# Eight weight pieces move to GpSimd's DMA queue, and one block of a matrix-vector product moves from TensorE to VectorE

## The chip, the cores and the metric

The kernel runs on one core of a Trainium2 chip. The metric is the device time of one execution in microseconds, as the median of three runs. All profiles are of one execution each.

## The reference, cut to what matters

The reference is one inference step of a two-layer network for two groups of tokens: 128 context tokens and 512 latent tokens, model width 2048, all in float32. Each layer does the following (the mixers, two kinds of attention and a gated convolution in the first layer, are left out here):

```python
def modulation(cond, w, b):                      # w: (2048, 6144)
    m = jax.nn.silu(cond) @ w + b
    return jnp.split(m, 3, axis=-1)              # shift, scale, gate

sh, sc, gt = modulation(c, ada_w[layer], ada_b[layer])
h = rms_norm(x, norm_g[layer]) * (1.0 + sc) + sh
out = mixer(h, ...)                              # begins with h @ w_in, w_in: (2048, 6656)
x = x + gt * out
```

There are two conditions, `c` for the latent tokens and `c_ctx` for the context tokens, so the modulation is a product of a 2 x 2048 matrix with 2048 x 6144 weights (48 MB for each layer), of which every weight is used once for each condition. `h` cannot be made before shift and scale of its rows are known.

## The kernel before

Tokens lie along the free axis (640 of them, `NT`), features on the 128 partitions, so a feature block of 128 rows of `h` is one tile `h0` to `h15`. Matmuls of the projections are split in three float32r products (`wh*hi`, `wh*lo`, `wl*hi`, lines 276 to 278); `split_w` makes `wh` on ScalarE (line 241) and `wl` on VectorE (line 242) from a loaded tile `raw`.

The modulation weights are cut in blocks of 512 columns (`cb`): blocks 0 to 3 are the shift, 4 to 7 the scale, 8 to 11 the gate. Block `g` and block `4 + g` belong to quarter `g` of the features (four `h` tiles). In layer 0 the shift and scale blocks are made by `ada_on_pe`: TensorE multiplies 16 slices of the block (line 178, `T<-ada,sT`), ScalarE copies the result (line 181), TensorE transposes it (line 184), VectorE reduces it and adds the bias (`red`, `mod`), and for a scale block makes `gsc` (line 144). The weights of a block come in two loads of 2 MB into two buffers `ada0` and `ada1`, on SyncE's queue (line 175). Block 5 is loaded otherwise: with `spare=range(8, 16)` it comes in eight pieces of 512 KB into the buffers of `h8` to `h15`, which hold no `h` yet (tile `adah`, line 165, also on SyncE's queue). Gate blocks and all of layer 1 are made by `ada_on_dve` later on: each step loads 128 rows (tile `adaw`, line 207, three buffers) and VectorE adds them, times the condition, into two accumulators (lines 211 and 213); at the end TensorE sums over the partitions with a matrix of ones (line 219), ScalarE copies (line 222), TensorE transposes (line 225), VectorE adds the bias.

The change lies in the lead stage of the first projection (`run_tiles` with `trans`). Six output tiles are worked on at once, and the features are gone through in six units: `cut` splits the first and the last quarter in two halves, so units 1 and 2 are quarter 1, units 3 and 4 are quarters 2 and 3, and units 5 and 6 the halves of quarter 4. In each unit `h0_maker` makes `h` (`ht<-xT,gsc,tables` at line 893, `hi` at 897, `lo` at 898), and then the six tiles follow. Four of them are summed over the units in SBUF on VectorE (`sum`, line 345), which also frees their PSUM bank; two stay in PSUM. At the second tile of each unit `ahead` calls `ada_group`, which makes the shift and scale blocks of the next unit:

```python
def ada_group(g, js):
    for cb in (4 + g, g):
        ada_on_pe(0, cb, js[0] // 2, js[1] - js[0], range(8, 16) if cb == 5 else ())
```

For the halves of a quarter a half of the block is made each time. A scheduler puts the recorded instructions in a fixed order on each engine before the run. An engine, and the queue of an engine that issues DMAs, takes its instructions strictly in that order.

Of the kernel before, what the change touches and what calls it, by code (L numbers as in the profile page):

```python
# [53 lines left out]
def trunk_kernel(ctx: ExitStack, tc: tile.TileContext, I: dict, O: dict):  # L54
    nc = tc.nc
    V, A, PE, G = nc.vector, nc.scalar, nc.tensor, nc.gpsimd
# [100 lines left out]
    def ada_on_pe(l, cb, h=0, n=4, spare=()):  # L157


        acc, m, wd = psT(), 2 if spare else 32 // n, n * P  # L160
        order, ws = list(range(KT)), []
        if spare:
            for i, s in enumerate(spare):
                w = hpool.tile([P, m, wd], F32, tag=f"h{s}", name="adah")
                nc.sync.dma_start(w, ada_src(l, cb, i * m, m))
                ws.append(w)

            order.reverse()
        for i, kt in enumerate(order):
            if spare:  # L170
                w = ws[kt // m]
            elif kt % m == 0:
                w = ada_t[0].rearrange("p (k n) -> p k n", k=m)
                ada_t.reverse()
                nc.sync.dma_start(w, I["ada_w"][l, kt * P:(kt + m) * P, cb * 512 + h * 256:cb * 512 + h * 256 + wd]
                                  .rearrange("(k p) n -> p k n", p=P))
            g = kt % 4
            PE.matmul(acc[32 * g:32 * g + 32, 0:wd], sT[:, kt, :], w[:, kt % m, :],  # L178
                      start=(i < 4), stop=(i >= KT - 4), tile_position=(0, 32 * g))
        sb = ada_sb  # L180
        A.copy(sb[:, 0:wd], acc[:, 0:wd])
        tr = psT()
        for j in range(n):
            PE.transpose(tr[:, j * P:(j + 1) * P], sb[:, j * P:(j + 1) * P], ident)
        red = small.tile([P, n, 2], F32, tag="red", name="red", bufs=2)
        V.tensor_reduce(red, tr[:, 0:wd].rearrange("p (b g c) -> p b c g", b=n, g=4)[:, :, 0:2, :], axis=AX.X,
                        op=ALU.add)
        add_bias(l, cb, red, h, n)
        ada_done(l, cb, h, n)
# [117 lines left out]
            credit[0] -= 1.0  # L307

    def run_tiles(jobs, w_ap, make_h, fill=None, rate=0.0, ahead=None, order=(0, 1, 2, 3), before=None,
                  last=None, by_half=False, trans=[], grace=0, cut=None, summed=None, led=None, fill_from=0, lead_in=None):  # L310
        if trans:
            lp = tc.tile_pool(name="lead", bufs=1, side="right")
            lead_pool = lp.__enter__()
            sums = {n: lead_pool.tile([P, NT], F32, name=f"sum{n}") for n in trans}
            held = [n for n in range(2 + len(trans)) if n not in trans]

            leads = [n for m in range(len(held) + 1) for n in trans[m:m + 1] + held[m:m + 1]]
            leads += trans[len(held) + 1:]
        else:
            leads, held, lp = list(range(min(3, len(jobs)))), [], None  # L320
        lead = len(leads)
        pps = {n: (sums[n][:, 0:HALF], sums[n][:, HALF:NT]) if n in trans
               else new_pp(1 + held.index(n) if trans else n) for n in leads}
        units = [(pos, qd, js) for pos, qd in enumerate(order) for js in (cut if cut and pos in (0, 3) else [(0, 4)])]
        for ui, (pos, qd, js) in enumerate(units):
            raws = {n: load_raw(w_ap, jobs[n][0], qd, js) for n in leads[:W_BUFS]}
            if ui == 0 and lead_in:
                lead_in()
            parts = {n: split_w(raws[n]) for n in raws}
            for hv in [HV[:1], HV[1:]] if by_half and pos == 0 else [HV]:  # L330
                for k in range(4 * qd + js[0], 4 * qd + js[1]):
                    make_h(k, hv) if by_half else make_h(k)
                for n in leads:
                    if ahead and n == leads[1] and ui + 1 < len(units):
                        ahead(*units[ui + 1][1:])
                    if n not in parts:
                        parts[n] = split_w(load_raw(w_ap, jobs[n][0], qd, js))
                    if n in trans:
                        pp = new_pp(0)
                        proj_q(pp, parts[n], qd, pos, alone=True, js=js)  # L340
                        for i, sl in HV:
                            if ui == 0:
                                A.copy(pps[n][i], pp[i][:, 0:HALF])
                            else:
                                V.tensor_add(pps[n][i], pps[n][i], pp[i][:, 0:HALF])
                        if summed:
                            summed(ui, n, pps[n])
                    else:
                        proj_q(pps[n], parts[n], qd, pos, hv, js=js)
                    advance(attn, 1)  # L350
        if led:
            led()

        quarters = [(col, qd) for col, _ in jobs[lead:] for qd in range(4)]
        raws, parts = {}, {}

        def run_ahead(t):
            for i in range(len(raws), min(t + RAW_AHEAD, len(quarters))):
                raws[i] = load_raw(w_ap, *quarters[i])
                j = len(parts)  # L360
                if j < t + SPLIT_AHEAD and j <= i:
                    parts[j] = split_w(raws[j])
            for j in range(len(parts), min(t + SPLIT_AHEAD, len(quarters))):
                parts[j] = split_w(raws[j])

        def begin(fn, pp):
            g = fn(pp)
            if g is not None:
                prep.append(g)
                advance(prep, 1)  # L370

        def settle():

            while pending:
                n = pending.pop(0)
                drain(prep)
                if before:
                    before(n)
                begin(jobs[n][1], pps[n])
            drain(prep)  # L380

        pending = list(range(lead))
        if lead == len(jobs):
            def go_on():
                if pending and not prep:
                    n = pending.pop(0)
                    begin(jobs[n][1], pps[n])
                slot()
                return pending or prep
            return go_on  # L390
        run_ahead(0)
        t = 0
        if before:
            settle()
        else:
            n = pending.pop(0)
            begin(jobs[n][1], pps[n])
        for i in range(lead, len(jobs)):
            fn = jobs[i][1]
            pp = new_pp((i - lead) % 2)  # L400
            split_last = last is not None and i == len(jobs) - 1
            for qd in range(4):
                proj_q(pp, parts[t], qd, qd, HV[:1] if split_last else HV)
                if before and qd == 0:
                    before(i)
                t += 1
                run_ahead(t)
                if pending and not prep:
                    n = pending.pop(0)
                    begin(jobs[n][1], pps[n])  # L410
                slot(fill, rate if t > fill_from else 0.0)
            if split_last:
                first = last(pp, 0)
                next(first)
                for qd in range(4):
                    proj_q(pp, parts[t - 4 + qd], qd, qd, HV[1:])
                    next(first, None)
                for _ in last(pp, 1):
                    pass
                return  # L420
            drain(prep)
            if i >= lead + grace and pending:
                settle()
            if lp and not pending and not prep:
                lp.__exit__(None, None, None)
                lp = None
            begin(fn, pp)
# [443 lines left out]
        A.copy(rows[:, bs[0] * P:(bs[-1] + 1) * P], t[:, 0:len(bs) * P])  # L871

    def ada_group(g, js):
        for cb in (4 + g, g):
            ada_on_pe(0, cb, js[0] // 2, js[1] - js[0], range(8, 16) if cb == 5 else ())
        if g == 3 and js[1] == 4:
            for i, n in enumerate(("a_k_norm", "c_k_norm", "d_k_norm")):
# [27 lines left out]
    def keep(ui, n, pp):  # L905
        g = {(4, 0): 0, (4, 4): 1, (5, 0): 2, (5, 4): 3}.get((ui, n))
        if g is not None:
            V.tensor_copy(xTm[g][:, 4 * NT:], pp[1][:, 0:1])
            nc.gpsimd.dma_start(x0dram[g], xTm[g])

    def even_start():
        close("start")
# [111 lines left out]
    for i in range(4, 8):  # L1024
# [2 lines left out]
    u0, c0, b0, h0, g0, g1 = jobs[4:10]  # L1027
    jobs[0:10] = [u0, jobs[0], jobs[1], g0, jobs[2], jobs[3], g1, c0, b0, h0]
    run_tiles(jobs, I["ev_w_in"][0], h0_maker, fill0, FILL0, ada_group, trans=TRANS, grace=GRACE, cut=((0, 2), (2, 4)),
              summed=keep, led=even_start, lead_in=lambda: ada_on_pe(0, 0, 0, 2))  # L1030
    drain(prep)
    for _ in fill0:
        pass
# [466 lines left out]
```

## Time and profile before

| | |
|---|---|
| Median of 3 runs | 2333.73 us (2332.94 to 2334.4) |
| The profiled execution | 2333.26 us, its span 2331.3 us |
| TensorE matmul busy | 2286.6 us, 98% |
| VectorE busy | 1572.5 us, 67% |
| ScalarE busy | 929.2 us, 40% |
| GpSimd busy | 133.0 us, 6% |
| Mean granted TensorE clock | 0.996 |

A line of the profile names an engine (PE is TensorE, PEld its weight loads, DVE VectorE, ACT ScalarE, POOL GpSimd, SP SyncE; SPq is SyncE's queue issuing a DMA), a source line, the operation, and the tile it writes and those it reads. A line in order of time begins with its start and its length in us and ends with the number of merged instructions and, in brackets, how long the engine was idle before it and what it waited for. Matmuls overlap, so their lengths add up to more than the time they take; 12 of them follow each other at 0.147 us.

### The profile page before, as it was taken

The numbers are of one execution on the slowest core, as the hardware profiler recorded it, in microseconds if no ns is written. First come the engines' busy times: TensorE is split into PE (matmuls) and PEld (weight loads), VectorE is DVE, ScalarE is ACT, GpSimd is POOL, SyncE is SP. The second block draws the span as 40 slices with busy tenths as digits, with TensorE's granted clock in tenths as the row PEclk, the third lists the DMA queues.
The fourth block names the chain that finished last, engine by engine and source line by source line (L and its number), as shares of the span: only waits on it lengthen the run. The fifth ranks groups of instructions, "written<-read, shape, count | busy, mean of one in ns | idle before, by whom it ended". The sixth has DMA issues, their size and how long they took to land.

```text
span 2331.3 us, 41439 instructions
## 1 busy us (share of the span) xinstructions
PE 2286.6 (98%) x15988; PEld 2210.0 (95%) x15988; DVE 1572.5 (67%) x3196; ACT 929.2 (40%) x1935; POOL 133.0 (6%) x181
## 2 busy tenths in 40 slices
PE   7999999999999999999999999999999999999999
PEld 5699999999999999999999999999999999999999
DVE  4559886786876663988855755755756754567576
ACT  4235442433422222544554344444334444444343
POOL 1001000000000000000010100101000001000101
PEclk9999999999999999999999999999999999999999
DMA  9984545445355443844431422413423312128642
GB/s 315 354 267 131 162 116 170 139 119 169 116 180 162 151 139 114 277 142 128 160 98 53 135 82 72 143 52 100 118 72 95 104 46 82 46 74 270 181 122 70
DMA packets 390630, 321.96 MB, mean 138 GB/s; under 512 B 18402, under 2 KB 336368, under 8 KB 389920
## 3 DMA queue, kind: packets, MB, share of 16 engines
q1 hardware_dynamic: 382496, 288.98, 40.9%
q0 software_dynamic: 7216, 28.16, 3.3%
q8 instruction: 126, 2.06, 0.4%
q10 hardware_dynamic: 720, 2.16, 0.3%
q14 instruction: 72, 0.59, 0.1%
HBM read 290.79 MB, written 28.44 MB: 137 GB/s over the span
## 4 chain that ended last, share of the span: by engine, by line
PE 88%; DMA 4%; DVE 4%; ACT 2%; issue 1%; POOL 0%; SPq 0%; ACTq 0%; DVEq 0%; POOLq 0%
PE pa L276 10%; PE pb L277 10%; PE pb L276 10%; PE pb L278 10%; PE pa L277 10%; PE pa L278 10%; PE pq L526 4%; PE pq L528 4%; PE pq L527 4%; PE T L704 2%; PE S L716 1%; PE S L718 1%; PE S L717 1%; DMA yin<-yd 1%; PE T L178 1%
## 5 line engine op out<-in xcount | busy, mean ns | idle before, releaser
L241 ACT ACTIVATE wh<-raw 128x512 fp32r<-128x512 f32 (+1 forms) x490 | 303.1, 620 | 794.7 <-PE pb L277 655.3
L242 DVE TENSOR_TENSOR wl<-raw,wh 128x512 fp32r<-128x512 f32 (+1 forms) x490 | 330.8, 676 | 351.3 <-ACT wh L241 326.1
L276 PE MATMUL pa<-h,wh 128*128 128x320 f32 x1760 | 560.6, 319 | 4.5 <-ACT h L241 3.2
L277 PE MATMUL pa<-h,wh 128*128 128x320 f32 x1760 | 547.3, 312 | 1.8 <-DVE h L242 1.8
L278 PE MATMUL pa<-h,wl 128*128 128x320 f32 x1760 | 546.4, 310 | 0.0
L278 PE MATMUL pb<-h,wl 128*128 128x320 f32 x1760 | 545.4, 310 | 0.0
L276 PE MATMUL pb<-h,wh 128*128 128x320 f32 x1760 | 545.0, 310 | 0.0
L277 PE MATMUL pb<-h,wh 128*128 128x320 f32 x1760 | 544.8, 310 | 0.0
L213 DVE SCALAR_TENSOR_TENSOR acc<-adaw,sT,acc 128x512 f32<-128x512 f32 (+1 forms) x600 | 357.4, 639 | 13.1 <-DMA adaw<-in_ada_w 12.4
L276 PEld LDWEIGHTS pa<-h,wh 128*128 128x128 f32 x1760 | 331.9, 189 | 24.0 <-issue 14.7
L277 PEld LDWEIGHTS pa<-h,wh 128*128 128x128 f32 x1760 | 332.6, 189 | 6.3 <-DVE h L242 2.7
L278 PEld LDWEIGHTS pa<-h,wl 128*128 128x128 f32 x1760 | 332.1, 189 | 1.2 <-issue 1.2
L278 PEld LDWEIGHTS pb<-h,wl 128*128 128x128 f32 x1760 | 330.8, 188 | 2.1 <-issue 2.1
L276 PEld LDWEIGHTS pb<-h,wh 128*128 128x128 f32 x1760 | 330.6, 188 | 1.0 <-issue 0.4
L277 PEld LDWEIGHTS pb<-h,wh 128*128 128x128 f32 x1760 | 330.8, 188 | 0.2
L690 ACT ACTIVATE p<-S,nm,rq 128x768 f32<-128x768 f32 (+3 forms) x120 | 101.2, 844 | 114.8 <-DVE nm L685 81.1
L526 PE MATMUL pq<-h,wh 128*128 128x320 f32 x352 | 110.0, 313 | 0.4 <-DVE xr L1083 0.4
L527 PE MATMUL pq<-h,wh 128*128 128x320 f32 x352 | 108.8, 309 | 0.0
L528 PE MATMUL pq<-h,wl 128*128 128x320 f32 x352 | 108.4, 309 | 0.0
L683 DVE TENSOR_REDUCE nm<-S 128x1 f32<-128x768 f32 (+3 forms) x120 | 91.9, 766 | 16.1 <-PE S L718 14.9
L241 ACT ACTIVATE pth<-T 128x512 fp32r<-128x512 f32 (+1 forms) x132 | 65.9, 533 | 71.4 <-PE T L704 71.3
L527 PE MATMUL pq<-T,wh 128*128 128x320 f32 x264 | 81.4, 308 | 0.0
(303 smaller groups left out, 3382.5 us busy)
## 6 DMA issues: line engine op xcount, KB each, us to landing
raw<-in_od_w_in SPq DMA_DIRECT2D x208, 256.0 KB, 2.8
raw<-in_ev_w_in SPq DMA_DIRECT2D x196, 256.0 KB, 3.0
adaw<-in_ada_w SPq DMA_DIRECT2D x192, 256.0 KB, 3.0
ada<-in_ada_w SPq DMA_DIRECT2D x14, 2048.0 KB, 11.0
adaw<-in_ada_w SPq DMA_DIRECT2D x128, 128.0 KB, 2.3
yd<-y POOLq DMA_DIRECT2D x34, 320.0 KB, 2.8
yin<-yd SPq DMA_DIRECT2D x32, 320.0 KB, 4.8
w<-yd SPq DMA_DIRECT2D x32, 320.0 KB, 4.4
```

Source lines behind the costliest of these rows:

```text
L213: V.scalar_tensor_tensor(out=a, in0=w, scalar=sT[:, kt, c:c + 1], in1=a, op0=ALU.mult, op1=ALU.add)
L241: A.activation(hi, x, AF.Copy)
L242: V.tensor_sub(lo, x, hi)
L276: PE.matmul(ps, wh[:, i, :], hi[:, sl], start=(j == js[0] if alone else (pos == 0 and j == 0)), stop=False)
L277: PE.matmul(ps, wh[:, i, :], lo[:, sl], start=False, stop=False)
L278: PE.matmul(ps, wl[:, i, :], hi[:, sl], start=False, stop=(j == js[1] - 1 if alone else (pos == 3 and j == 3)))
L526: PE.matmul(ps, wh[:, j, :], hi, start=(h == 0 and j == 0), stop=False)
L527: PE.matmul(ps, wh[:, j, :], lo, start=False, stop=False)
L528: PE.matmul(ps, wl[:, j, :], hi, start=False, stop=(h == 1 and j == 3))
L683: V.tensor_reduce(nm, s, axis=AX.X, op=ALU.max, negate=True)
L690: A.activation(p[:, 0:n], s, AF.Exp, scale=rsc, bias=nm, accum_out=l)
L704: PE.transpose(t[:, i * P:(i + 1) * P], p, ident)
```

## The change

Three things are changed. First, `ada_on_pe` issues the eight pieces of block 5 on GpSimd's queue instead of SyncE's, and in front of each stands a copy of one column on VectorE, from the modulation of feature block 18 (the scale of the first quarter's second half) into the piece's buffer; the DMA overwrites that column, so it cannot start before that scale is known. Second, for the last quarter `ada_group` no longer calls `ada_on_pe` for block 7 (the scale), only for block 3 (the shift). Third, block 7 is made by `ada_on_dve` in 32 steps of 128 rows by 256 columns, with buffers in the pool of the opening; `run_tiles` takes three steps of it behind each of the six tiles of units 3 and 4.

```diff
@@ ada_on_pe
                 w = hpool.tile([P, m, wd], F32, tag=f"h{s}", name="adah")
-                nc.sync.dma_start(w, ada_src(l, cb, i * m, m))
+
+                V.tensor_copy(w[:, 0, 0:1], mod[0][:, 18, 0:1])
+                nc.gpsimd.dma_start(w, ada_src(l, cb, i * m, m))
@@ run_tiles, with a new argument by_lead=None, behind each tile of a unit
                     advance(attn, 1)
+                    if by_lead:
+                        by_lead(ui)
@@ ada_group
-        for cb in (4 + g, g):
+        for cb in (4 + g, g)[g == 3:]:
             ada_on_pe(0, cb, js[0] // 2, js[1] - js[0], range(8, 16) if cb == 5 else ())
@@ before the first projection
+    lead_fill = ada_on_dve([(0, 7)], ("acc0", "acc1", "adaw", "adaw", "adaw", "adaw"), 2)
+
+    def lead_steps(ui):
+        for _ in range(3 if ui in (2, 3) else 0):
+            next(lead_fill, None)
...
-              summed=keep, led=even_start, lead_in=lambda: ada_on_pe(0, 0, 0, 2))
+              summed=keep, led=even_start, lead_in=lambda: ada_on_pe(0, 0, 0, 2), by_lead=lead_steps)
```

More of the change, by code (lines that the diff above doesn't have):

```diff
@@ L309, in run_tiles @@
     def run_tiles(jobs, w_ap, make_h, fill=None, rate=0.0, ahead=None, order=(0, 1, 2, 3), before=None,
-                  last=None, by_half=False, trans=[], grace=0, cut=None, summed=None, led=None, fill_from=0, lead_in=None):
+                  last=None, by_half=False, trans=[], grace=0, cut=None, summed=None, led=None, fill_from=0, lead_in=None, by_lead=None):
         if trans:
```

## Prediction

> **What bounds the kernel now.** I read the page first, then the busy time by stretches of the opening, then SyncE's queue and TensorE in order of time there.
>
> ```profile
> span 2331.3 us, 41439 instructions
> ...
> PE 88%; DMA 4%; DVE 4%; ACT 2%; issue 1%; POOL 0%; SPq 0%; ACTq 0%; DVEq 0%; POOLq 0%
> ```
>
> TensorE carries 88% of the chain that ended last, so what the change adds to or takes from TensorE's path early on stays to the end. Behind the lead stage both programs have the same instructions in the same order on every engine, so only the lead stage (to about 165 us) can differ. The profiled execution took 2333.26 us, 1.96 us around its span; the median of the three runs is 2333.73, 0.47 above it.
>
> ```profile
> 46.00:50.00 4.00, 4.00 (x47) 3.29 (x49) 2.81 (x7) 1.78 (x5) 0.00 (x0) 1.00 0.10 32
> 66.00:74.00 8.00, 3.08 (x24) 1.12 (x28) 2.47 (x7) 0.76 (x2) 0.00 (x0) 0.95 1.08 375
> 82.00:100.00 18.00, 18.00 (x122) 11.75 (x121) 9.85 (x23) 3.72 (x7) 0.00 (x0) 1.00 0.85 305
> 100.00:120.00 20.00, 20.00 (x154) 16.19 (x150) 12.34 (x26) 8.32 (x17) 0.00 (x0) 1.00 1.06 340
> 120.00:140.00 20.00, 20.00 (x157) 18.84 (x157) 9.59 (x24) 4.90 (x11) 0.00 (x0) 1.00 0.83 259
> ```
>
> The columns are length, busy time of PE, PEld, DVE, ACT and POOL, granted clock, DMA share and GB/s. From 46 to 50 the DMA engines stand nearly idle (0.10); from 66 to 74 they are full and TensorE works 3.08 of 8 us. From 82 to 140 TensorE has no idle time, and VectorE is busy 9.85 + 12.34 + 9.59 = 31.8 of 58 us.
>
> ```profile
> 41.98 0.70 SPq L165 DMA_DIRECT2D adah<-in_ada_w  x1
> 48.75 0.88 SPq L254 DMA_DIRECT2D raw<-in_ev_w_in  x2
> 49.69 3.65 SPq L165 DMA_DIRECT2D adah<-in_ada_w  x7
> 53.43 5.00 SPq L175 DMA_DIRECT2D ada<-in_ada_w  x2
> ```
>
> This is why: piece 1 goes out at 41.98, then SyncE's queue stands at a `raw` load until 48.75, and pieces 2 to 8 and both loads of shift block 1 wait behind it.
>
> ```profile
> 62.24 3.64 PE L178 MATMUL T<-adah,sT 128*32 128x512 f32 x32
> ...
> 68.23 1.92 PE L178 MATMUL T<-ada,sT 128*32 128x512 f32 x16 [0.93 <-DMA ada<-in_ada_w]
> ...
> 73.50 3.44 PE L178 MATMUL T<-ada,sT 128*32 128x512 f32 x16 [3.34 <-DMA ada<-in_ada_w]
> ```
>
> The second half of shift block 1 lands last: TensorE waits 3.34 us for it, and then the same 16 records take 3.44 us where they took 1.92 at 68.23: after such a wait the clock is low, at a cost of 1.5 us.
>
> **Part 1, the pieces on GpSimd's queue.** In the changed order SyncE's queue goes from the loads before it straight to shift block 1's first half, and the pieces leave on GpSimd's queue as soon as VectorE's eight one-column copies are done, which stand right behind the scale `gsc` of the first quarter's second half (45.58 us, quoted below) and behind the four `ht` operations that follow it: two pieces at about 46, six at about 48 to 52.
>
> ```profile
> 142.33 0.15 DVE L908 COPY xT<-sum 128x1 f32<-128x1 f32 x1
> ```
>
> ```profile
> 142.77 0.59 POOL L909 DMA_DIRECT2D x0d<-xT x1 [115.32 <-DVE xT L908]
> ```
>
> Eight copies by 0.15 are 1.2 us of VectorE ahead of the splits `wl` of the second unit; TensorE is busy 4.00 of 4.00 us there and afterwards waits for data until 73.5, so I cost them at nothing (1.2 us if that cover goes). Eight issues by 0.59 are 4.7 us of GpSimd, behind which nothing stands before the write at 142.77. The transfers then fill the hole from 46 to 50: the same bytes up to shift block 1 end up to 4 x 0.90 = 3.6 us earlier, and if the wait shrinks, up to 1.5 us of slow clock goes too: a gain of at most 5.1. The lower bound comes from loads that share the engines with GpSimd's queue:
>
> ```profile
> DMA to landing us min/median/max: 5.7/5.8/5.8
> ```
>
> ```profile
> DMA to landing us min/median/max: 2.8/3.1/3.6
> ```
>
> The first line is of `raw` loads issued from 160 to 165 us, while the writes of `x0d` run on GpSimd's queue, the second of those from 196 to 240, without them: 2.7 us more each. So the next unit's loads and shift block 1 can come that much later than in one queue, a loss of 2.7. The trace of before has no loads of this size on two queues at once, so between +2.7 and -5.1 I take **-2.0**: the hole is certain, but TensorE takes the pieces before shift block 1 (3.64 us), and what has arrived early in block 1 is of no use until the last piece is there. The Trainium skill, "DMA: Bandwidth & Descriptors" (Queues, rings and completion order), says that each DMA engine takes turns between the queues that have work, a packet at a time. The two landing times above agree; by that rule pieces and block 1 finish together, about when block 1 finished alone, and this term would be 0 instead of -2.0.
>
> **Part 2, block 7 off TensorE.**
>
> ```profile
> 141.48 1.93 PE L178 MATMUL T<-ada,sT 128*32 128x256 f32 x32
> ...
> 144.03 0.38 PE L184 MATMUL T<-ident,ada_sb 128*128 128x128 f32 x2
> ```
>
> One half of a block is 1.93 + 0.38 = 2.31 us of TensorE, on the path; both halves of block 7 are **-4.6**. (The second one stands here, in the fifth unit, with shift block 3's second half behind it.)
>
> **Part 3, the 64 accumulations and their place.**
>
> ```profile
> 1321.54 1.67 DVE L213 SCALAR_TENSOR_TENSOR acc<-adaw,sT,acc 128x256 f32<-128x256 f32 x4
> ```
>
> ```profile
> DMA to landing us min/median/max: 2.0/2.3/3.0
> ```
>
> These are four operations of the same shape later in this kernel, and the landing of their 128 KB loads (1283 to 1320 us): 0.42 us each, 0.84 a step, 27 us in all. There are three load buffers, so the load of step n waits until step n-3 is done, and takes 2.3 us: at best three steps in about 3.5 us. The loads stand in SyncE's queue between the others: three before scale block 6, the fourth only behind shift block 2's second half, whose issue waits until TensorE has read block 6:
>
> ```profile
> 91.60 1.92 PE L178 MATMUL T<-ada,sT 128*32 128x512 f32 x16
> ```
>
> So 29 steps remain from 93 or 94, at best 10 rounds of 3.5, and two 2 MB loads of block 3 stand between them. VectorE's fixed order puts steps 1 to 26 ahead of the last sums of the fourth unit, and **steps 27 to 32 behind them**. Before the change block 7 was ready early and unit 5 followed unit 4 without a gap. Now TensorE ends unit 4 and waits for: the last sum, three steps, the load for the last one, that step, then the combination.
>
> ```profile
> 45.17 0.17 DVE L186 TENSOR_REDUCE red<-T 128x4 f32<-128x16 f32 x1 [5.30 <-PE T L184]
> 45.38 0.16 DVE L155 TENSOR_TENSOR mod<-red,vec 128x4 f32<-128x4 f32 x1
> 45.58 0.16 DVE L144 SCALAR_TENSOR_TENSOR gsc<-mod,vec 128x4 f32<-128x4 f32 x1
> 45.78 1.94 DVE L893 SCALAR_TENSOR_TENSOR ht<-xT,gsc,tables 128x512 f32<-128x512 f32 x4
> ```
>
> ```profile
> 241.21 0.64 PE L219 MATMUL T<-acc,ones 128*32 128x256 f32 x8
> ...
> 241.94 0.37 ACT L222 COPY ada_sb<-T 128x256 f32<-128x256 f32 x1 [0.15 <-PE T L219]
> ...
> 242.47 0.38 PE L225 MATMUL T<-ident,ada_sb 128*128 128x128 f32 x2
> ```
>
> ```profile
> L897 ACT ACTIVATE h<-ht,mod 128x512 fp32r<-128x512 f32 x16 | 11.5, 718 | 9.7 <-DVE mod L155 5.2 <-DVE ht L893 4.5
> L893 DVE SCALAR_TENSOR_TENSOR ht<-xT,gsc,tables 128x512 f32<-128x512 f32 x14 | 10.5, 748 | 0.2
> L345 DVE TENSOR_TENSOR sum<-sum,pb 128x320 f32<-128x320 f32 x20 | 9.7, 485 | 5.9 <-PE pb L278 5.9
> ```
>
> The first four rows are VectorE's in order of time; the next three a combination of the same code at 241 us; the last three are groups (busy us, mean ns of one).
>
> Sum 0.49 + three steps 2.5 + landing 2.3 + last step 0.84 = 6.1; ones 0.64, copy 0.37, transpose 0.38, from the reduction to `ht` 45.78 - 45.17 = 0.6, `ht` 0.75, `h` 0.72 = 3.5; some 0.4 between them: 10.0 us. In it TensorE has only block 3's second half, which it had to do anyway (2.3): 10.0 - 2.3 = 7.7, and after so long a wait 1.5 of slow clock, as at 73.50: **+9.2**. Its bounds are 7.1 (the loads are there already and the clock stays up: 0.5 + 12 operations by 0.42 + 3.9 - 2.3) and 12.7 (the last load lands after 5.8 instead of 2.3 us, as the `raw` loads beside another queue's traffic did).
>
> Ahead of it VectorE gets 26 steps by 0.84 = 22 us on top of its 31.8 of 58, in groups of three that wait for their loads, with sums, splits and the next `h` queued behind them; a sum frees the bank into which TensorE's next tile goes, and the low halves of `h` gate the fourth unit. Each group can hold TensorE up by up to its 2.5 us or not at all. There are seven groups between 95 and 140, and I see three or four at a place where a sum or an `h` would be next. The bounds are 0 and 8; nearest is half: **+4.0**. SyncE's 32 more issues stand among its waits, and the last `raw` loads behind them have two units of lead; nothing added.
>
> **Sum**: -2.0 - 4.6 + 9.2 + 4.0 = +6.6, on 2333.26 gives 2339.9, on the median 2340.3; I say **2340**. About 0.2% (4.7 us) is what a measurement of this kernel can tell from no change.
>
> **Rivals.**
> *Cover holds.* The hole is filled with full effect (-5.1) and only one or two groups hold TensorE up (+2): -5.1 - 4.6 + 9.2 + 2 = +1.5, 2335. For it speaks that the DMA engines are the bound until 74; against it, VectorE's order.
> *Faster.* The early loads are the whole bound: all idle time from 66 to 74 (8 - 3.08 = 4.9) and 1.5 of clock go, no group waits, and TensorE meets block 3 so late in its wait that the clock stays up (tail 7.7): -4.9 - 1.5 - 4.6 + 7.7 = -3.3; it decides once some 2.3 us of weight loading between 82 and 100 (11.75 of 18) also come back: -5.6, 2328. Against it: the wait behind unit 4 has no other work.
> *Two queues in turn.* By the landing times above the second unit's `raw` loads and shift block 1 come later (+2.7), the 2 MB loads delay the steps, and the tail is 2 longer: +2.7 - 4.6 + 11.2 + 4 = +13.3, 2347. It is the skill's rule of turns taken further than I take it.
> That the change doesn't act as described (pieces still late, since they now wait for `gsc`) would leave part 1 at 0: within my forecast's range.
>
> **How the numbers follow.** Forecast 0.52 (2335 to 2345, of which 0.06 lies within 4.7 us of before), cover holds 0.24, faster 0.09, queues in turn 0.15. Slower by over 0.2%: 0.46 + 0.15 = 0.61; within: 0.06 + 0.24 = 0.30; faster: 0.09. The range leaves out the faster case and the far end of the last: 2331 to 2348.
>
> **What would show it.** In the profile after: the DMA share from 46 to 50 near 1; the wait at the second half of shift block 1 shorter than 3.34; a TensorE wait of 6 to 9 us at about 140 ended by the chain `acc`, `T`, `mod`, `ht`, `h`, with low clock behind it; VectorE waits for `adaw` between 95 and 140. I am wrong if TensorE goes from unit 4 to unit 5 with no gap, if VectorE never holds a sum up, or if the opening gains more than 5 us.

## The result, and the profile after

| | before | after |
|---|---|---|
| Median of 4 runs | 2333.34 us (2327.84 to 2334.4) | 2347.31 us (2344.94 to 2349.81) |
| Profiled execution, its span | 2333.26, 2331.3 | 2344.94, 2343.2 |
| Ratio of the times | 1 | 1.0065, 95% interval 1.0045 to 1.0084 |

The change costs 15 us (10.5 to 19.6 by the interval). The forecast was 2340 with a range of 2331 to 2348: slower, as forecast, but by more than twice the 6.6 us of the sum. The profiled pair differs by 11.9 us of span; the profiled execution after is the fastest of its four.

I read the stretches first, as for the kernel before (length, busy time of PE, PEld, DVE, ACT and POOL, granted clock, DMA share, GB/s).

```profile
46.00:50.00 4.00, 4.00 (x48) 2.85 (x47) 1.68 (x7) 1.70 (x5) 3.95 (x7) 1.00 1.05 405
66.00:74.00 8.00, 8.00 (x66) 4.07 (x59) 4.17 (x12) 3.16 (x6) 0.00 (x0) 1.00 0.79 221
100.00:120.00 20.00, 16.57 (x105) 12.39 (x103) 17.31 (x40) 7.51 (x14) 0.00 (x0) 0.94 0.95 291
120.00:140.00 20.00, 19.23 (x134) 16.89 (x134) 14.71 (x39) 3.15 (x7) 0.00 (x0) 0.98 0.68 211
140.00:150.00 10.00, 3.29 (x25) 3.02 (x24) 8.44 (x23) 0.42 (x1) 0.00 (x0) 0.91 0.43 125
150.00:160.00 10.00, 9.54 (x63) 5.25 (x64) 6.61 (x20) 3.21 (x7) 0.07 (x1) 0.75 0.00 0
```

The hole from 46 to 50 is filled (0.10 became 1.05), and TensorE no longer idles from 66 to 74. But from 100 to 120 VectorE is busy 17.31 of 20 us and TensorE loses 3.4 us, and from 140 to 150 TensorE works 3.29 of 10 us, followed by a stretch at a clock of 0.75.

**The opening**, TensorE and then SyncE's queue and VectorE in order of time:

```profile
63.54 3.64 PE L180 MATMUL T<-adah,sT 128*32 128x512 f32 x32 [0.73 <-DMA adah<-in_ada_w]
...
68.52 3.64 PE L180 MATMUL T<-ada,sT 128*32 128x512 f32 x32
72.92 0.66 PE L186 MATMUL T<-ident,ada_sb 128*128 128x128 f32 x4
...
76.77 0.41 PE L278 MATMUL pa<-h,wh 128*128 128x320 f32 x1 [1.58 <-DVE sum L347]
```

```profile
68.93 0.92 SPq L256 DMA_DIRECT2D raw<-in_ev_w_in  x2
69.91 0.97 SPq L209 DMA_DIRECT2D adaw<-in_ada_w  x2
70.92 21.29 SPq L177 DMA_DIRECT2D ada<-in_ada_w  x4
```

```profile
74.26 1.28 DVE L215 SCALAR_TENSOR_TENSOR acc<-adaw,sT,acc 128x256 f32<-128x256 f32 x3 [1.54 <-DMA adaw<-in_ada_w]
75.46 0.18 DVE L188 TENSOR_REDUCE red<-T 128x8 f32<-128x32 f32 x1
```

Both halves of shift block 1 are there when the pieces have been used: no wait of 3.34 any more. But the first steps of block 7 stand on VectorE ahead of block 1's reduction and wait 1.54 us for their loads, and TensorE then waits 1.58 us for a sum. Scale block 6's first load goes out at 70.92, behind a raw pair and two step loads; before it went out at 70.21.

**Units 3 and 4**, VectorE and then TensorE around one hold-up:

```profile
110.40 2.46 DVE L215 SCALAR_TENSOR_TENSOR acc<-adaw,sT,acc 128x256 f32<-128x256 f32 x6 [0.48 <-DMA adaw<-in_ada_w]
112.78 0.48 DVE L347 TENSOR_TENSOR sum<-sum,pa 128x320 f32<-128x320 f32 x1
113.17 0.48 DVE L347 TENSOR_TENSOR sum<-sum,pb 128x320 f32<-128x320 f32 x1
113.57 1.89 DVE L244 TENSOR_TENSOR wl<-raw,wh 128x512 fp32r<-128x512 f32 x3
115.38 1.94 DVE L902 SCALAR_TENSOR_TENSOR h<-ht,mod,h 128x512 fp32r<-128x512 f32 x4
```

```profile
113.31 0.42 PE L278 MATMUL pa<-h,wh 128*128 128x320 f32 x1 [0.57 <-DVE sum L347]
...
116.18 0.41 PE L279 MATMUL pa<-h,wh 128*128 128x320 f32 x1 [2.05 <-DVE h L902]
```

Three steps (2.46 us) stand in front of the last sums of unit 3; behind those come the splits and only then the low halves of `h`, for which TensorE waits 2.05 us.

**Behind unit 4**, VectorE and then TensorE:

```profile
143.29 0.49 DVE L347 TENSOR_TENSOR sum<-sum,pb 128x320 f32<-128x320 f32 x1 [0.35 <-PE pb L280]
144.65 2.46 DVE L215 SCALAR_TENSOR_TENSOR acc<-adaw,sT,acc 128x256 f32<-128x256 f32 x6 [0.87 <-DMA adaw<-in_ada_w]
...
147.78 2.53 DVE L215 SCALAR_TENSOR_TENSOR acc<-adaw,sT,acc 128x256 f32<-128x256 f32 x6 [0.34 <-DMA adaw<-in_ada_w]
```

```profile
149.97 1.46 PE L221 MATMUL T<-acc,ones 128*32 128x256 f32 x6 [6.71 <-DVE acc L215]
151.89 0.69 PE L227 MATMUL T<-ident,ada_sb 128*128 128x128 f32 x2 [0.46 <-ACT ada_sb L224]
152.51 2.68 PE L180 MATMUL T<-ada,sT 128*32 128x256 f32 x18
```

This is the wait that was forecast: last sum, steps, load, steps, sums over the partitions. Its parts differ: the forecast had four steps and one landing of 2.3 us, the trace has six steps and 1.21 us of waiting for loads. The ones took 1.46 us for six, where eight took 0.64 with the clock up; the granted clock was 0.50 from 150 to 154 us.

**The path measured between the same instructions.** Before, then after, TensorE; and the last sum of unit 4 of before (that of after stands above):

```profile
44.75 0.38 PE L184 MATMUL T<-ident,ada_sb 128*128 128x128 f32 x2
...
106.21 0.60 PE L184 MATMUL T<-ident,ada_sb 128*128 128x128 f32 x4
...
149.47 0.31 PE L276 MATMUL Sp<-h,wh 128*128 128x320 f32 x1
```

```profile
42.79 0.38 PE L186 MATMUL T<-ident,ada_sb 128*128 128x128 f32 x2
...
104.16 0.66 PE L186 MATMUL T<-ident,ada_sb 128*128 128x128 f32 x4 [0.76 <-ACT ada_sb L183]
...
162.25 0.31 PE L278 MATMUL Sp<-h,wh 128*128 128x320 f32 x1
```

```profile
139.83 0.49 DVE L345 TENSOR_TENSOR sum<-sum,pb 128x320 f32<-128x320 f32 x1 [1.27 <-PE pb L278]
```

The first row of each is the first quarter's second scale, ahead of the first piece on GpSimd's queue (44.53): after stands 1.96 us earlier there, which no moved piece can have caused (run 10, with the opening of the kernel before up to here, has this row at 43.03), so I count from it. Then: shift block 2, 61.46 before and 61.37 after (-0.1); from there to unit 4's last sum 33.62 and 39.13 (+5.5, with 2.31 of block 7 gone: hold-ups of **7.8**); from there to the held tile `Sp` of unit 5 9.64 and 18.96 (+9.3, again with 2.31 gone: **11.6**). In all +14.7 at `Sp`; less the 1.96 that is 12.8, and 11.9 are left at the end.

The -0.1 is one profile's reading. Run 14, whose edit acts only later, took 63.14 us for the same stretch (+1.7), so this term is known to some 2 us. The 7.8 are what is left over when block 7 is taken off: TensorE stood idle for 3.4 us of them and had a granted clock of 0.96 in that stretch (0.50 from 118 to 120 us, behind the wait for `h`), which is another 1.6; the rest I can't place.

### The profile page after: what moved, and what is told of

It reads as the page before. It is cut to its first block, busy times and chain, and to the rows that moved or that the text cites. A ratio compares the mean times of both kernels' runs of the same rounds, so it can differ in the third digit from the quotient of the medians.

```text
span 2343.2 us, 41477 instructions
## 1 busy us (share of the span) xinstructions
PE 2286.5 (98%) x15930; PEld 2207.8 (94%) x15930; DVE 1594.9 (68%) x3265; ACT 928.5 (40%) x1934; POOL 139.2 (6%) x189
## 3 DMA queue, kind: packets, MB, share of 16 engines
q8 instruction: 125, 2.05, 0.4%
## 4 chain that ended last, share of the span: by engine, by line
PE 52%; DVE 3%; ACT 1%; DMA 1%; issue 1%; POOL 0%; SPq 0%; POOLq 0%; DVEq 0%; ACTq 0%
PE pb L279 5%; PE pb L278 5%; PE pa L278 5%; PE pb L280 5%; PE pa L280 5%; PE pa L279 5%; PE pq L530 4%; PE pq L532 4%; PE pq L531 4%; PE T L708 1%; PE S L720 1%; PE S L722 1%; PE S L721 1%; PE T L559 1%; DMA adaw<-in_ada_w 1%; PE T L769 1%
## 5 line engine op out<-in xcount | busy, mean ns | idle before, releaser
L215 DVE SCALAR_TENSOR_TENSOR acc<-adaw,sT,acc 128x512 f32<-128x512 f32 (+1 forms) x660 | 383.4, 627 | 24.5 <-DMA adaw<-in_ada_w 23.3
L278 PEld LDWEIGHTS pa<-h,wh 128*128 128x128 f32 x1760 | 331.3, 188 | 28.8 <-issue 12.8
L244 DVE TENSOR_TENSOR ptl<-T,pth 128x512 fp32r<-128x512 f32 (+1 forms) x132 | 77.8, 610 | 5.7 <-ACT pth L243 4.3
```

The source lines that it names most:

```text
L215: V.scalar_tensor_tensor(out=a, in0=w, scalar=sT[:, kt, c:c + 1], in1=a, op0=ALU.mult, op1=ALU.add)
L244: V.tensor_sub(lo, x, hi)
L278: PE.matmul(ps, wh[:, i, :], hi[:, sl], start=(j == js[0] if alone else (pos == 0 and j == 0)), stop=False)
```

## The experiments

Gains and losses in us are the ratio to the kernel before, times 2333. Each theory carries the numbers that were read from the trace after.

**Run 1: part 1 alone.** Block 7 back on TensorE:

```diff
-        for cb in (4 + g, g)[g == 3:]:
+        for cb in (4 + g, g):
...
-              ..., by_lead=lead_steps)
+              ...)
```

> Only part 1 of the change: the eight pieces on GpSimd's queue with the one-column copies; block 7 is back on TensorE. Theory (the loss lies in where VectorE's order puts the steps of block 7): the opening gains as after the change, shift block 1 ready some 4.8 us earlier (72.9 instead of 77.7), of which 1.9 us are left at shift block 2 (105.3 instead of 107.2); the end follows: 2331.4, 1.9 under before. Rival (the pieces beside SyncE's queue cost time behind the opening, by contention): 2336 to 2340, above before.

Measured: ratio 1.001 (0.9999 to 1.002), +2.3 us. The theory's -1.9 fell: part 1 alone gains nothing. The time, 2335.3 by the ratio, is just under the rival's 2336. Its profile, TensorE, SyncE's queue, and the stretch from 70 to 80; then the same stretch and the queue of the kernel before:

```profile
65.38 5.34 PE L180 MATMUL T<-adah,sT 128*32 128x512 f32 x32 [3.71 <-DMA adah<-in_ada_w]
...
86.14 1.89 PE L180 MATMUL T<-ada,sT 128*32 128x512 f32 x2 [3.08 <-DMA ada<-in_ada_w]
```

```profile
72.21 0.92 SPq L256 DMA_DIRECT2D raw<-in_ev_w_in  x2
...
74.04 23.68 SPq L177 DMA_DIRECT2D ada<-in_ada_w  x4
```

```profile
70.00:80.00 10.00, 10.00 (x79) 6.38 (x72) 6.30 (x17) 4.43 (x10) 0.00 (x0) 1.00 0.57 156
```

```profile
70.00:80.00 10.00, 6.66 (x42) 3.62 (x39) 3.45 (x9) 3.48 (x7) 0.00 (x0) 0.83 1.08 379
```

```profile
70.21 1.08 SPq L175 DMA_DIRECT2D ada<-in_ada_w  x1
```

Before, block 1's first half landed at 68.1 us and its second at 73.4 (issue plus time to landing, here and below). The first was read while TensorE waited for the second, so its buffer was free, and block 6's load went out at 70.21: the share from 70 to 80 was 1.08. With the pieces on a second queue both halves of block 1 land earlier (54.8 and 68.7), but the last piece, which TensorE needs first, lands at 65.2 instead of 61.6. It is now waited for (3.71 us), the granted clock behind that wait is low (0.72 from 65 to 71 us), and TensorE reads both halves of block 1 only from 72.05 on, one right behind the other. So the first buffer comes free later, block 6 goes out at 74.04, and the share is 0.57. TensorE then waits 3.08 us at block 6. The hole in the transfers was not closed; it moved. In the change's own profile the wait for the last piece was only 0.73 us; in runs 3 and 14 it was 4.15 and 4.55. Run 9 tests this.

**Run 2: block 7 alone**, pieces on SyncE's queue, no copies:

```diff
-                V.tensor_copy(w[:, 0, 0:1], mod[0][:, 18, 0:1])
-                nc.gpsimd.dma_start(w, ada_src(l, cb, i * m, m))
+                nc.sync.dma_start(w, ada_src(l, cb, i * m, m))
```

> Only parts 2 and 3: block 7 on VectorE, the pieces back on SyncE's queue without the copies. Theory: -4.6 of TensorE, +7.9 of hold-ups to the end of unit 4, +11.5 behind it: +14.8, 2348. Rival (part of the loss comes from the pieces' queue): +6 to +9, 2339 to 2342.

Measured: 1.0066 (1.0053 to 1.0079), +15.4. The theory's number; the rival fell. Block 7 costs as much alone as the whole change.

**Run 3: half of VectorE's work.**

```diff
+                    if c and kt and cb == 7 and l == 0:
+                        continue
```

> The change with half of VectorE's work for block 7: the second condition's accumulator gets only its first step, 30 of the 64 operations are left out; loads, places and waits stay. Theory (VectorE's own work in front of sums and h): the hold-ups go from 7.9 to 3 or 4 and the wait behind unit 4 gets 2.5 shorter (six operations by 0.42): 2339 to 2341, 7 under after. Rival (VectorE stands waiting for the steps' loads, three buffers on SyncE's queue): the loads land when they did, 2345 to 2347.

Measured: 1.0038 (1.0026 to 1.005), +8.9, some 6 under the change. The total is close to the theory's, but the trace gives each side one place. The hold-ups from shift block 2 to unit 4's last sum fell from 7.8 to 4.3. From there to `Sp` it was 18.83 us, as long as in the change (18.96): with less work VectorE stood longer for loads. What VectorE waited for ahead of these steps from 95 to 165 us (us, times), in this run and then in the change:

```profile
  DMA adaw<-in_ada_w: 15.0, 13
```

```profile
  DMA adaw<-in_ada_w: 4.9, 5
```

So ahead of unit 4's end VectorE's work is the cost, and behind it the loads through three buffers are at least as slow as the work. In this profile the whole path from the first quarter's second scale to `Sp` is only 1.7 us shorter than in the change (117.74 and 119.46), and its time, 2343.43, is the longest of its runs: the trace does not place all of the 6 us.

**Run 4: the steps spread over units 2, 3 and 4.**

```diff
-        for _ in range(3 if ui in (2, 3) else 0):
+        for _ in range(2 if ui in (1, 2, 3) else 0):
```

> The change with the steps taken two behind each tile of units 2, 3 and 4 instead of three behind each tile of units 3 and 4: the last step and gsc then stand ahead of the last sums of unit 4. Theory: the wait of 6.7 us behind unit 4 goes, with the 11.5 it cost; hold-ups stay at about 8 to 10: -2 - 4.6 + 9 = +2.5, 2336 (2334 to 2338). Rival (loads): the steps' loads now lie in the stretches where the DMA engines are full, shift block 1 and scale block 6 come later, and what is won behind unit 4 is lost ahead of unit 3: 2343 to 2347.

Measured: 1.0028 (1.0019 to 1.0037), +6.5: between the two. TensorE has no wait behind unit 4 any more (the ones at 144.30 follow without a gap), but block 6's transpose comes 55.50 us after the first quarter's second scale instead of 49.53: part of the gain is lost in the opening, where the rival had it. The rival's reason, the loads, isn't shown: at 84.22 TensorE waits 2.27 us for an `h` whose `ht` VectorE began only at 83.39, with accumulations, sums and splits ahead of it.

**Run 5: wide loads.** Four steps in one load, into the buffers of `h12` to `h15`:

```diff
+                    if i % 4 == 0:
+                        w4 = hpool.tile([P, 4, wd], F32, tag=f"h{12 + i // 4 % 4}", name="adaw")
+                        nc.sync.dma_start(w4, ...)        # 512 rows by 256 columns
+                    w = w4[:, i % 4, :]
```

> The change with the loads of block 7's steps made four steps at a time (512 KB), into the four buffers of h12 to h15, which are free until unit 5: eight loads on SyncE's queue instead of 32, and up to 16 steps loaded ahead instead of three. VectorE's order then has the steps in smaller groups, with gsc ahead of the last sums of unit 4. Theory 1 (the loads pace the steps, and with them the wait behind unit 4): the 11.5 behind unit 4 go, the hold-ups fall to about 4: 0 - 4.6 + 4, 2332 (2330 to 2335). Theory 2 (27 us more of VectorE's work hold TensorE up wherever they stand): the hold-ups of about 8 stay and the block's end is only less late: 2336 to 2340.

Measured: 1.0051 (1.0038 to 1.0063), +11.9; both expectations missed. There is no wait behind unit 4 here either, but TensorE waits 2.03 and 2.35 us for `wh` and `wl` at 106.85 and 110.53. That `wh` stands on ScalarE behind an `h` that waited for the shift, and that `wl` on VectorE behind eleven accumulations (4.44 us from 105.44), which had come in one run after VectorE had waited 6.66 us for a load of the steps. One place's wait became another's.

**Run 6: part 1 alone, block 6 on GpSimd's queue too.**

```diff
-                nc.sync.dma_start(w, I["ada_w"][...])
+                (nc.gpsimd if (l, cb) == (0, 6) else nc.sync).dma_start(w, I["ada_w"][...])
```

> Part 1 alone (as in the run with the pieces only), and the two loads of scale block 6 on GpSimd's queue too. Theory (the opening's gain is given back at block 6, whose first load now stands behind two raw loads that wait on SyncE's queue, 74.0 instead of 70.2 us): the wait of 3.1 us at block 6 and the 1.7 of slow clock behind it go: 2329 to 2331, 3 to 5 under the run with the pieces only. Rival (pieces on a second queue cost by contention, at block 6 as well): no difference from the run with the pieces only, 2333 to 2336.

Measured: 1.0038 (1.0025 to 1.005), +8.9: worse than run 1, against both. VectorE and then TensorE in this run, and the landing of the `raw` loads issued from 66 to 80 us (min, median, max):

```profile
83.39 0.17 DVE L906 TENSOR_SCALAR nsink<-sink 128x8 f32<-128x8 f32 x1 [7.02 <-DMA sink<-in_a_sink]
83.47 0.48 DVE L347 TENSOR_TENSOR sum<-sum,pb 128x320 f32<-128x320 f32 x1
```

```profile
84.00 0.64 PE L278 MATMUL pb<-h,wh 128*128 128x320 f32 x1 [6.47 <-DVE sum L347]
```

```profile
DMA to landing us min/median/max: 2.9/3.5/13.7
```

VectorE's order here has a small operation, `nsink`, ahead of a sum. Its load `sink` goes out on SyncE's queue at 73.73, beside block 6's two loads, and lands after 9.6 us (6.3 in the kernel before, where it goes out at 131.94); the sum stands behind it, and TensorE waits 6.47 us. Of the `raw` loads one, issued at 75.67 beside block 6, lands after 13.7 us, the others after 2.9 to 3.9; it lands at 89.4, when TensorE has long gone on, so it isn't what the 6.47 us are made of. The DMA share from 76 to 84 was 0.93, so there was little room beside block 6. The profile is the fastest of ten runs (2334.04, median 2339.87), so the 8.9 us aren't all in it.

**Run 7: part 1 alone without the copies** (the line with `V.tensor_copy` left out).

> Part 1 alone without the eight one-column copies: the pieces leave on GpSimd's queue as soon as the buffers of h8 to h15 are free, not behind the first quarter's second scale. Theory (block 6 sets the start of unit 3): the wait for the last piece (3.7 us) goes and shift block 1 is ready earlier, but block 6 lands when it did: 2332 to 2335, no gain. Rival (the opening up to shift block 1 is the bound): 2328 to 2331. If the early pieces delay the loads of units 1 and 2, TensorE waits for raw before 60 us and the time is above 2336.

Measured: 1.0016 (1.0006 to 1.0026), +3.7, no better than run 1. The pieces go out at 14.03, 25.23 and from 27.29 us on, and TensorE waits ahead of shift block 0:

```profile
41.79 3.64 PE L179 MATMUL T<-ada,sT 128*32 128x256 f32 x32 [8.39 <-DMA ada<-in_ada_w]
```

The load it waits for was issued at 22.3 us and landed after 19.3; in the kernel before the same load, issued at 21.2, landed after 12.5. The copies are what keeps the pieces from taking the engines from block 0's loads.

**Run 8: the steps' loads on GpSimd's queue.**

```diff
-                nc.sync.dma_start(w, I["ada_w"][l, kt * P:(kt + 1) * P, c0:c0 + wd])
+                (nc.gpsimd if (l, cb) == (0, 7) else nc.sync).dma_start(w, ...)
```

> The change with the 32 loads of the steps on GpSimd's queue instead of SyncE's, three buffers as before. Theory 1 (places in SyncE's queue: the steps' loads stand behind raw loads that wait, and delay block 6 and raw themselves): the steps come earlier, gsc stands ahead of unit 4's last sums, the wait behind unit 4 goes: 2333 to 2337. Theory 2 (three buffers and the landing time of 2 to 3 us pace the steps on any queue): the wait behind unit 4 stays at 5 us or more, 2343 to 2347.

Measured: 1.0042 (1.003 to 1.0055), +9.8; between the two. VectorE's order has many steps early, and from shift block 2 to `Sp` it takes 40.7 us, 2.6 less than before: no hold-up and no wait, and part of the 4.6 comes through. But the steps now stand on VectorE from the first unit on and wait there for their loads (2.65, 0.65 and 2.37 us between 33 and 44 us): TensorE waits 7.05 us for an `h` at 45.51, and shift block 1 is transposed at 85.09 instead of 77.71.

**Run 9: part 1 alone, block 6 in pieces** in the buffers of `h8` to `h15`, on SyncE's queue:

```diff
-            ada_on_pe(..., range(8, 16) if cb == 5 else ())
+            ada_on_pe(..., range(8, 16) if cb in (5, 6) else ())
...
+                if cb == 5:
                     V.tensor_copy(w[:, 0, 0:1], mod[0][:, 18, 0:1])
-                nc.gpsimd.dma_start(w, ...)
+                (nc.gpsimd if cb == 5 else nc.sync).dma_start(w, ...)
```

> Part 1 alone, and scale block 6 loaded like block 5: eight pieces in the buffers of h8 to h15, on SyncE's queue, so its loads no longer wait until TensorE has read shift block 1 out of its two buffers. Theory (the hole in the transfers has only moved: with two queues in turn block 5 and both halves of block 1 arrive together, the buffers come free together, and between 70 and 80 us the DMA share falls from 1.08 to 0.57): the share there is above 0.9, the wait of 3.1 us at block 6 and its 1.7 of slow clock go: 2330 to 2332, some 3 to 4 under the run with the pieces only. Rival (what part 1 loses is lost by late raw loads beside the second queue): 2334 to 2336, as before this edit.

Measured: 0.9982 (0.9974 to 0.9991), 4.2 us **under** the kernel before and 6.5 under run 1. Its stretch from 70 to 80, and TensorE at block 6:

```profile
70.00:80.00 10.00, 10.00 (x77) 8.06 (x70) 8.58 (x20) 4.31 (x9) 0.00 (x0) 1.00 0.92 310
```

```profile
84.79 3.64 PE L181 MATMUL T<-adah,sT 128*32 128x512 f32 x32
```

The share is 0.92 and nothing waits at block 6. The theory of the moved hole holds, and this version beats both kernels.

**Run 10: the kernel before with block 6 in pieces** (the first line of that edit alone).

> The kernel before, with scale block 6 in pieces as in the run above and nothing else. Theory: before, the first half of block 1 is read 5 us ahead of the second, block 6's load starts at 70.2 us and no wait stands at block 6, so there is nothing to win: 2331 to 2333. Rival (block 6's buffers bind in the kernel before, too): 2328 to 2330.

Measured: 0.9993 (0.9983 to 1.0003): no difference that can be told, as the theory has it. Only part 1 and the pieces of block 6 together gain by more than the noise; the intervals of runs 9 and 10 still overlap a little.

**Run 11: the loads of block 7 without its work.**

```diff
+                    if kt and cb == 7 and l == 0:
+                        continue
```

> The change with all of block 7's loads, but with four of the 64 accumulations; 60 operations are left out. VectorE's order is then almost that of before, and gsc is ready early. Theory (VectorE's own work and its order make the loss, as half the work gave 6 us back): no hold-up and no wait behind unit 4, the 4.6 of TensorE come through, part 1 gives 0 to +2: 2328 to 2331. Rival (the 32 loads on SyncE's queue hold up raw and block 6, whatever VectorE does): 2335 to 2339.

Measured: 0.9994 (0.9985 to 1.0004), -1.4. Sixty accumulations less, some 25 us of VectorE, are worth 16.6 us; the 32 loads alone cost little (-4.6 for block 7 and +2.3 from run 1 make -2.3, and -1.4 came). The rival fell.

**Run 12: run 9 without the copies.**

> The run with block 6 in pieces on SyncE's queue, without the one-column copies: block 5's pieces leave on GpSimd's queue from the first. Theory: as with the copies, the moved hole is filled: 2330 to 2333, and no wait at block 6. Rival (early pieces take the engines from the first loads of x and block 0: TensorE stood 8.4 us at 41 us in the run without copies): that delay stays and is paid in full, 2335 to 2338.

Measured: 1.001 (1.0 to 1.0019), +2.3. TensorE again waits 8.64 us ahead of shift block 0; the rival holds, and the copies are worth 6.5 us here.

**Run 13: the whole change with run 9's edit.**

> The whole change, and scale block 6 loaded in eight pieces on SyncE's queue, as in the run that did so with part 1 alone. Theory (the two losses add: the moved hole costs some 6.5 us with part 1 alone, block 7 costs the rest): 2341 to 2343, 5 to 6 under the change. Rival (in the change VectorE's steps set the pace of units 3 and 4, and an earlier block 6 only waits longer for them): 2345 to 2348.

Measured: 1.0053 (1.0041 to 1.0066), +12.4, 2.8 under the change with overlapping intervals. It isn't the 5 to 6 of the theory; by the ratio, 2345.4, it is at the lower end of the rival's band. In this profile, as in the change's, TensorE waits for a sum, not for block 6, at the start of unit 3 (0.80 and 1.58 us). Whether anything is gained stays open.

**Run 14: 26 of the 32 steps.**

```diff
+                if (l, cb) == (0, 7) and i >= 26:
+                    continue
```

> The change with the last six of block 7's 32 steps left out, loads and accumulations: VectorE's order is that of the change up to the last sums of unit 4, and there the sums over the partitions and gsc stand ahead of the last sum instead of two groups of steps behind it. Theory (the wait behind unit 4 is worth the 11.5 us read from the trace, hold-ups ahead of it stay at 7.8): 2335 to 2337, 10 to 12 under the change. Rival (the combination of the block is the larger part of that wait): 2341 to 2343, the 5 us of the six steps alone.

Measured: 1.0061 (1.0048 to 1.0075), +14.2: a miss for both. From the first quarter's second scale to `Sp` of unit 5 the path is 112.46 us, 7.0 shorter than in the change (119.46). But then, TensorE and SyncE's queue of this run:

```profile
176.79 0.61 PE L280 MATMUL pa<-h,wh 128*128 128x320 f32 x1 [6.00 <-DVE sum L349]
```

```profile
143.53 16.06 SPq L258 DMA_DIRECT2D raw<-in_ev_w_in  x6
159.64 0.92 SPq L907 DMA_DIRECT2D tables<-in_k_tables  x1
161.27 24.77 SPq L258 DMA_DIRECT2D raw<-in_ev_w_in  x9
```

The new `tables` go out as soon as the last `ht` of the lead stage has read the old ones, and the `raw` loads of the next tiles stand behind that load (147.02 in the kernel before, 159.64 here). The first three behind it land after 6.3 to 11.6 us, behind `tables` (768 KB) and beside the writes of `x0d`, with the DMA share at 1.04 from 165 to 175, and TensorE waits 6.00 us for them. In the change itself `tables` goes out at 164.00, the loads behind it land after 3.5 to 7.0 us, and TensorE waits 1.08 us at that place. So 4.9 of the 7.0 us were given back 20 us later, and of the rest the times show at most 1 us (+14.2 and +15.2, with overlapping intervals).

## Why the prediction was wrong, step by step

**Signs.** The DMA share from 46 to 50 (1.05), the wait at block 1's second half (gone), the wait behind unit 4 (6.71 us, chain as listed, clock 0.75 behind it) and VectorE's waits for `adaw` all came as said. So both places where VectorE holds TensorE up were named rightly, and both were priced too low; part 1, a gain in the prediction, was none. The range held; the sum, +6.6 for a measured +15.2, did not.

| term | forecast | the change's trace | runs |
|---|---|---|---|
| part 1 | -2.0 | -0.1 (run 14: +1.7) | +2.3 alone (run 1) |
| block 7 off TensorE | -4.6 | -4.6 | |
| VectorE holds TensorE up | +4.0 | +7.8 | 4.3 with half the work (run 3) |
| wait behind unit 4 | +9.2 | +11.6 | |
| sum | +6.6 | +14.7 | +15.2 |

**Part 1** is the step that failed in kind. Its gain was taken at shift block 1 and carried to the end. It was there (from the scale to block 1's transpose 30.13 us after, 32.96 before: 2.8), and by block 6's transpose it was gone (49.76 after, 49.53 before). I had not followed the buffers of block 1 on to block 6, nor priced that the last piece lands later when block 1 shares the engines with it, nor seen that VectorE's first steps would stand ahead of block 1's reduction; my seven groups began at 95 us. Runs 9 and 10 show the step to block 6: with its load taken off those two buffers, part 1 gains 4.2 us.

The Trainium skill, "DMA: Bandwidth & Descriptors" (Queues, rings and completion order), says that each DMA engine takes turns between the queues that have work. The trace agrees: block 1's first half on SyncE's queue, issued at 42.23, landed at 55.5, between the first piece on GpSimd's queue (51.6) and the last (63.4). But the 0 that I had worked out from this rule came about in another way: I had block 1 finish when it did alone, and its second half landed at 67.6 instead of 73.4; what was won there was lost again at block 6.

**Hold-ups**: I took half of a bound of 0 to 8, and 7.8 came, the upper end. This and the wait behind unit 4 are the terms that were too small: together 19.4 us instead of 13.2. Run 11, with all the loads and four of the 64 accumulations, loses nothing, so both terms go back to VectorE's work. "Nearest is half" had no row behind it. A group held up not only a sum but also the splits and low halves of `h` queued behind it, and the wait was followed by a low clock (0.87 from 110 to 120). Half the work brought the term down to 4.3 (run 3).

**Behind unit 4**: 10.0 us were forecast for it, less 2.3 of block 3 and with 1.5 of slow clock. Until the ones begin it was 149.97 - 143.29 = 6.7 us (forecast 6.1); the rest is the combination at a granted clock of 0.50, which I had priced by rows at full clock (the ones 1.46 instead of 0.64, block 3's second half 2.68 for 18 matmuls instead of 1.93 for 32). "SyncE's 32 more issues: nothing added" was about right for their traffic (run 11), but with VectorE's work halved the loads through three buffers were as slow as the work (run 3). What run 14 adds is the next limit, `raw` behind `tables`.

**Rivals.** "Two queues in turn" had the time (2347) with two of its terms: a tail of 11.2 and a queue that takes turns. Its +2.7 for a later block 1 did not come, block 1 was earlier; the hold-ups were larger instead. That its time fits is in good part luck.

## What to carry to other kernels

When a transfer is moved into a hole of the DMA engines, ask which transfer the engine needs first, and follow its buffers to the next load that waits for them. Here the transfer that was needed first landed later on the second queue (65.2 instead of 61.6 us), the buffers behind it came free later, and the hole reappeared at the next load. Work moved to an engine that is "busy half of the time" is to be priced at the places where the fixed order puts it, and with all that is queued behind it. A wait priced from rows at full clock needs the slow clock in all that follows, and the next limit behind it (here `raw` behind `tables`) should be known before its removal is counted as a gain.

## What the runs showed of the hardware that I had not expected

The landing of `raw` loads on SyncE's queue that were issued from 46 to 56 us, before and then after (min, median, max):

```profile
DMA to landing us min/median/max: 2.2/2.5/2.9
```

```profile
DMA to landing us min/median/max: 11.4/13.6/18.9
```

Before, they went out to engines that were nearly idle (DMA share 0.10). After, they stand behind block 1's first half (2 MB, issued at 42.23) in their own queue and run beside the pieces on GpSimd's, and these two lines don't tell which of the two made them late; the issue of the slowest alone took 8.5 us. With one queue it is no better: in the kernel before, the `raw` loads issued from 58.5 to 67.3 us, behind the pieces and block 1, landed after 8.3 to 15.3 us. So in these traces a load that is issued behind or beside megabytes lands late on either arrangement, and the second queue only changed which transfers those were.

Eight loads of 512 KB were issued on GpSimd in 5.90 us, 0.72 to 0.79 each, where I had reckoned 0.59 from the writes of `x0d`, which are larger (1280 KB). And the same 32 matmuls of block 5 took 5.34 us after a wait of 3.71 us (run 1; granted clock 0.72 from 65 to 71) and 3.64 after one of 0.73 (the change).
